# Latent values kept on chip, three units' values as fill, values stored in reading order

## The chip, the cores and the metric

The kernel is one program on one core of a Trainium2 chip. The metric is device time in microseconds (us); each kernel is run several times and the median is given. A matrix engine (TensorE, PE), a vector engine (VectorE, DVE), a scalar engine (ScalarE, ACT), a general engine (GpSimd, POOL) and a queue for transfers (SyncE, SP) each run their own instructions in order and wait for each other by semaphores; GpSimd issues transfers too. Tiles lie in on-chip memory, matmul results in 8 PSUM banks, everything else in DRAM.

## The reference, cut to what matters

Two networks run one after the other on 512 tokens of width 1024. The change touches the first, which has two layers. Each layer computes three kinds of attention from one projection, gates them and adds them:

```python
for l in range(DEPTH):                       # 2
    h = rms_norm(x, g_mix[l])
    proj = h @ w_in[l]
    c_q, c_kv, k_r, qkv_b, qkv_c, gate_logits = jnp.split(proj, IN_SPLITS, axis=-1)
    y_a = mla_mixer(c_q, c_kv, k_r, g_q[l], g_kv[l], w_uq[l], w_ukv[l])      # latent, 8 heads
    ...
    y_b = dilated_mixer(q_b, k_b, qkv_b[:, :, 2])                            # 3 groups of 4 heads
    ...
    y_c = neighbourhood_mixer(qkv_c[:, :, 0], qkv_c[:, :, 1], qkv_c[:, :, 2], rpb[l])   # 8 heads
    gates = jax.nn.sigmoid(gate_logits...).reshape(B, S, N_BRANCH, D_MODEL)
    merged = (gates[:, :, 0] * (y_a @ w_pa[l]) + gates[:, :, 1] * (y_b @ w_pb[l])
              + gates[:, :, 2] * (y_c @ w_pc[l]))
    x = x + merged @ w_o[l]
    h = rms_norm(x, g_ffn[l])
    x = x + (jax.nn.silu(h @ w1[l]) * (h @ w3[l])) @ w2[l]
```

In the latent mixer keys and values are products of a normed vector of 128 numbers per token, `kv = (rms_norm(c_kv, g_kv) @ w_ukv)`. The dilated mixer attends within a band over every 1st, 4th or 16th token. The neighbourhood mixer lays the tokens out as a grid of 8 rows and 64 columns; each query sees 8 rows by 16 columns of keys and adds a bias by relative place (`rpb`).

## The kernel before, in words

All products are made in three passes of a split in high and low parts (`mm3`, L264 to L268): high by high, high by low, low by high. `weights` (L255 to L262) loads 512 KB of weights on SyncE into one of two tiles `wst`, ScalarE copies the high part `whi`, the vector engine subtracts the low part `wlo` (three of each). `split` (L245 to L253) does the same for any tile: one ScalarE copy, one vector subtraction, here with a factor per row of tokens where one is needed.

Heads come in pairs. A "unit" is two pairs: units 0 to 2 are the dilated groups, 3 and 4 the neighbourhood heads. `unit` computes queries and keys of a pair (`put` splits and reorders them into eight `qk` tiles of 512 columns; copies of keys to the other half of the rows are GpSimd transfers, L551) and loads the pair's values into a tile V (two of them) by `v_load`. The values of all five units are made by `v_tokens`: units 0 and 1 in products of 512 columns in four banks (mm, mm, mm, T), units 2 and 3 likewise in banks T, S, S, O, unit 4 in products of 256 columns. Each block of 128 tokens by 256 columns is split into a tile `vn` and stored to DRAM (`vd`) on GpSimd's queue:

```python
vn = self.t(self.tp, "vn", (P, 4, 2, 64), F32R, bufs=2)
self.split(vn[:, :, 0], vn[:, :, 1], ps.rearrange("p (h d) -> p h d", h=4), scale)
self.nc.gpsimd.dma_start(out=dst, in_=vn.rearrange("p h x d -> p (h x d)").bitcast(F32))
```

The latent values go the same way through `vn` to `vda` (L751) and come back by `v_load` (L761) on SyncE. For the neighbourhood pairs `v_load` is eight transfers, one for each half of 32 grid columns by 4 grid rows.

`branches` sets the order. `latent` is the projection and roots of the latent mixer and its values; it is woven with `values` (all of `v_tokens`): `weave(main, fill, ratio)` takes from fill as much cost as the main yields times the ratio, and PAUSE (31000, 10000) in the main lets that much fill pass at two places, while the roots are computed. Then `stream` runs seven stretches of attention groups (latent pairs 0 to 2, latent pair 3, dilated 0 to 2, neighbourhood 0 and 1). A group is a score, a turn (the transposes of E, split into `ph` and `pl`) and a value product, and these follow each other with the lags LAG. The fill of a stretch is the next unit's queries and keys, then GATES[i] gates (products of 1024 by 128 weights, stored to `td` by SyncE), in the proportion `fills[i] / mains[i]`. The tile scheduler keeps this order on each engine.

The largest negated score of a row, `nmx`, and the row sum, `den`, are two small tiles; `stat_rows` (L499 to L513) transposes each of them on PE, copies it into `row`, and stores it, so that `inverse` can read the sums back spread over 64 rows (L524). The bias tables of a neighbourhood pair are three transfers per head (L1011).

## Time and profile before

| | |
|---|---|
| runs | 2510.02 us median of 3 (2508.36 to 2512.51) |
| profiled execution | 2510.62 us, of which the span of instructions is 2508.9 |
| mean granted clock of TensorE | 0.966 |
| instructions | 31833 |

The profile is of one execution. The windows divide it by time: latent starts of the two layers lie at 75 to 125 and 1050 to 1100 us, the neighbourhood stages at 375 to 525 and 1340 to 1490. In a window one sees how long each engine was busy in it and which share of its full clock the chip granted TensorE; 0.50 is 1.2 GHz, 1.0 is 2.4 GHz. The waits name the engine and line that waited and what ended the wait. A timeline row is one instruction with its start, its duration, and in brackets the idle time before it.

### The profile page before, as it was taken

Reading aid. Unit: us, or ns where it says so; the run is one execution under the profiler, and the core shown is the slowest. Engines: PE = TensorE matmul, PEld = TensorE weight load, DVE = VectorE, ACT = ScalarE, POOL = GpSimd, SP = SyncE. Lnnn points to the kernel's source line nnn. Section 1 sums busy time; section 2 is a strip of 40 time slices with the busy share of each in tenths; the row PEclk is TensorE's granted clock in tenths of the full one; section 3 lists DMA queues with packets and bytes.
Section 4 is the critical chain, followed back from the end, with each engine's and each line's share of the span. In section 5 each row is a group of like instructions: output and inputs, shape, how many; then the busy total and the mean of one; then the engine's idle time right before and its main releaser. Section 6 shows DMA issues by size and latency. Waiting matters only on the chain. (4 is left out here: it accounts for less than half of the span.)

```text
span 2508.9 us, 31833 instructions
## 1 busy us (share of the span) xinstructions
PE 2347.2 (94%) x11200; PEld 1937.8 (77%) x11200; DVE 1561.6 (62%) x2387; ACT 1171.0 (47%) x2072; POOL 724.0 (29%) x837
## 2 busy tenths in 40 slices
PE   8699998799999999889998889999999899979996
PEld 7588887588888888678887668878888788858874
DVE  6477787466444333567877657677433676697666
ACT  5366775344323223355776544323222466435653
POOL 3224355423111100224444623211112122142214
PEclk9799999799999999989999889999999999989998
DMA  5455556465333344454545556786334332224222
GB/s 188 162 167 137 158 148 174 155 214 190 104 96 98 94 138 130 139 186 136 175 138 159 172 178 203 231 267 224 125 113 147 107 108 83 86 90 123 73 80 76
DMA packets 147822, 362.00 MB, mean 144 GB/s; under 512 B 21104, under 2 KB 48528, under 8 KB 147664
## 3 DMA queue, kind: packets, MB, share of 16 engines
q1 hardware_dynamic: 124368, 300.36, 38.2%
q0 software_dynamic: 23296, 59.62, 7.8%
q8 instruction: 88, 1.44, 0.2%
q14 instruction: 70, 0.57, 0.1%
HBM read 286.78 MB, written 45.86 MB: 133 GB/s over the span
## 5 line engine op out<-in xcount | busy, mean ns | idle before, releaser
L248 ACT ACTIVATE whi<-wst 128x1024 fp32r<-128x1024 f32 (+4 forms) x387 | 374.0, 967 | 675.0 <-PE mm L267 179.5
L249 DVE TENSOR_TENSOR wlo<-wst,whi 128x1024 fp32r<-128x1024 f32 (+4 forms) x387 | 462.7, 1196 | 310.5 <-ACT whi L248 302.4
L266 PE MATMUL mm<-hh,whi 128*128 128x512 f32 x1184 | 473.3, 400 | 20.7 <-ACT whi L248 19.6
L268 PE MATMUL mm<-hh,wlo 128*128 128x512 f32 x1184 | 469.9, 397 | 0.3 <-DVE wlo L249 0.2
L267 PE MATMUL mm<-hl,whi 128*128 128x512 f32 x1184 | 468.4, 396 | 0.0
L266 PEld LDWEIGHTS mm<-hh,whi 128*128 128x128 f32 x1184 | 225.4, 190 | 64.8 <-ACT whi L248 20.5
L268 PEld LDWEIGHTS mm<-hh,wlo 128*128 128x128 f32 x1184 | 225.2, 190 | 48.3 <-DVE wlo L249 2.3
L267 PEld LDWEIGHTS mm<-hl,whi 128*128 128x128 f32 x1184 | 225.5, 190 | 43.7 <-issue 0.2
L699 POOL TENSOR_TENSOR s<-s,rf 128x512 f32<-128x512 f32 x44 | 75.5, 1718 | 401.0 <-ACT s L698 401.0
L363 PE MATMUL T<-ident,E 128*128 128x128 f32 x768 | 119.0, 277 | 16.8 <-DVE row L512 5.7
L363 PEld LDWEIGHTS T<-ident,E 128*128 128x128 f32 x768 | 93.4, 142 | 39.2 <-issue 8.9
L339 PE MATMUL S<-qk,qk 128*128 128x512 f32 (+2 forms) x512 | 110.8, 335 | 12.6 <-DVE nmx L346 12.0
L248 ACT ACTIVATE ph<-T 128x512 fp32r<-128x512 f32 x160 | 94.1, 596 | 57.1 <-PE T L363 55.7
L534 POOL DMA_DIRECT2D ry<-tmp x136 | 67.9, 505 | 137.6 <-ACT tmp L531 69.8
L249 DVE TENSOR_TENSOR pl<-T,ph 128x512 fp32r<-128x512 f32 x128 | 86.9, 681 | 24.1 <-ACT ph L248 23.7
L339 PEld LDWEIGHTS S<-qk,qk 128*128 128x128 f32 x512 | 81.1, 196 | 22.4 <-DVE nmx L346 13.2
L415 POOL TENSOR_TENSOR O<-O,ll 64x256 f32<-64x256 f32 x72 | 75.8, 1053 | 69.7 <-DVE O L414 68.1
L300 POOL TENSOR_TENSOR tmp<-tmp,tmp 128x512 f32<-128x512 f32 x26 | 42.1, 1619 | 171.8 <-ACT tmp L296 168.1
L348 ACT ACTIVATE E<-E,nmx 128x256 f32<-128x256 f32 (+1 forms) x160 | 72.8, 456 | 38.8 <-DVE nmx L346 38.4
L266 PE MATMUL S<-hh,whi 128*128 128x512 f32 x208 | 82.9, 398 | 5.8 <-ACT hh L251 5.8
L268 PE MATMUL S<-hh,wlo 128*128 128x512 f32 x208 | 82.6, 397 | 2.7 <-DVE wlo L249 2.7
L267 PE MATMUL S<-hl,whi 128*128 128x512 f32 x208 | 82.7, 398 | 0.0
(629 smaller groups left out, 5472.4 us busy)
## 6 DMA issues: line engine op xcount, KB each, us to landing
wst<-win SPq DMA_DIRECT2D x153, 512.0 KB
wst<-w SPq DMA_DIRECT2D x120, 512.0 KB
mw<-wada SPq DMA_DIRECT2D x48, 512.0 KB
td<-gate SPq DMA_DIRECT2D x48, 256.0 KB
vd<-vn POOLq DMA_DIRECT2D x40, 256.0 KB, 2.3
qk<-qk POOLq DMA_DIRECT2D x80, 128.0 KB, 3.5
V<-vd SPq DMA_DIRECT2D x80, 128.0 KB
ry<-tmp POOLq DMA_DIRECT2D x136, 64.0 KB, 3.7
```

The costliest lines, as they stand in the source:

```text
L248: nc.scalar.activation(hi, src, AF.Copy)
L249: nc.vector.tensor_tensor(lo, src, hi.bitcast(F32), op=ALU.subtract)
L266: mm(out, ah, bh, start=start, stop=False, **kw)
L267: mm(out, ah, bl, start=False, stop=False, **kw)
L268: mm(out, al, bh, start=False, stop=stop, **kw)
L300: self.nc.gpsimd.tensor_tensor(new, acc, sq, op=ALU.add)
L339: nc.tensor.matmul(sp[:, i * nk:(i + 1) * nk], a, b, start=n == 0, stop=n == len(ops) - 1)
L348: nc.scalar.activation(e[:, sl], e[:, sl], AF.Exp, scale=-1.0, bias=m, accum_out=d)
L363: nc.tensor.transpose(tp[:, i * P:(i + 1) * P], e[:, i * P:(i + 1) * P], self.ident)
L415: nc.gpsimd.tensor_tensor(dst, dst, lo, op=ALU.add)
L534: nc.gpsimd.dma_start(out=y[r:r + 32], in_=f[r ^ 32:(r ^ 32) + 32])
L699: nc.gpsimd.tensor_tensor(s, s, r, op=ALU.mult)
```

## The change

- The latent values are split straight into the two V tiles on chip, scaled by r3's column, from banks S, S, T, O. The tile holds pairs 0 and 1, or 2 and 3. There is no `vda`.
- Units 0 and 1 are still made first, 512 columns wide, and are stored as one block of 128x1024 per 128 tokens, through the `ph` and `pl` tiles. Units 2, 3 and 4 are made 256 columns wide; what the latent main does not use up is the first fill of stretch 0, whose `fills` grows by 26000. PAUSE and GATES change.
- Unit 2's values are stored in the order in which dilation 16 reads them, units 3 and 4's by grid column; keys of the neighbourhood units are ordered by grid column too, and so are the bias tables and masks, so that the 32 columns that a block of queries sees are one run of 256. The V loads become one or two per pair, on GpSimd's queue.
- A bias table is one transfer of 128x768 per head, prepared by the host in that order.
- `qk` tiles hold high and low parts together, so that a key copy is one transfer where two were. `nmx` and `den` are one tile `stats`; a dilated pair transposes and stores both at once. `spread` is a helper for transfers that were written out before.
- The square sums of r2 and r3 use bank O instead of mm.

```diff
-GATES = (3, 0, 6, 1, 1, 4, 1)
+GATES = (1, 0, 6, 1, 1, 4, 3)
-PAUSE = (31000, 10000)
+PAUSE = (12000, 9000)
...
     def stat_rows(self, stat, order, dst):
-        ps = self.bank("ms")
+        ps, n = self.bank("ms"), stat.shape[1]
...
+    def spread(self, out, d, offset):
+        for j in range(2):
+            self.nc.gpsimd.dma_start(out=out[64 * j:64 * j + 64], in_=bass.AP(d.tensor, d.offset + offset + j * S, [[0, 64], [1, S]]))
...
     def v_tokens(self, win, rc, vd):
...
-        for base, units, tags in ((24, (0, 1), ("mm", "mm", "mm", "T")), (28, (2, 3), "TSSO")):
...
+            self.v_store(ps[tk], rc()[:, tk:tk + 1], vd[sl[tk], 0:1024], "p" + "hl"[tk % 2])
+        for u in (2, 3, 4):
+            wt = [self.weights(win[24 + 2 * u + c]) for c in range(2)]
+            for tk in range(4):
...
+                    self.mm3(ps, self.hh[:, k, sl[tk]], self.hl[:, k, sl[tk]], wt[k // 4][0][:, o], wt[k // 4][1][:, o],
+                             k == 0, k == 7)
+                    yield 330
+                dst = at(8 * tk * w + 512 * u, (w, 8), (32 * w, 16), (1, 512)) if u == 2 else \
+                    at(2 * tk * w + 512 * u, (w, 2), (8 * w, 64), (1, 512))
+                self.v_store(ps, rc()[:, tk:tk + 1], dst, "vn")
...
-                self.nc.sync.dma_start(out=(v[:, s:s + i + cnt] if cnt > 1 else v[:, s + i]).bitcast(F32), in_=src)
+                self.nc.gpsimd.dma_start(out=(v[:, s:s + i + cnt] if cnt > 1 else v[:, s + i]).bitcast(F32), in_=src)
...
-            vd = st["vd"] = self.t(self.dr, "vda", (S, 1024), bufs=1)
+            vs = st["v"] = [self.t(self.tp, "V", (P, 8, 256), F32R, bufs=2) for _ in range(2)]
             for tk in range(4):
-                ps = self.bank("mm")
+                ps = self.bank("SSTO"[tk])
...
-                for hf in range(2):
-                    self.v_store(ps[:, hf * 256:hf * 256 + 256], rc3[:, tk:tk + 1], vd[sl, hf * 512:hf * 512 + 512])
-                yield 1500
+                for i, v in enumerate(vs):
+                    hi, lo = (v[:, 2 * tk:2 * tk + 2].rearrange("p n (j x d) -> p (n j) x d", j=2, x=2)[:, :, x] for x in range(2))
+                    self.split(hi, lo, ps[:, i * 256:i * 256 + 256].rearrange("p (h d) -> p h d", h=4), rc3[:, tk:tk + 1])
+                yield 650
...
-        cparts = [(2 * w_, [(64, 4), (1, 32)], (256, 2), KC0[w_]) for w_ in range(4)]
+        colrow = lambda ap: ap.rearrange("p (r c) -> p c r", r=8)
...
+                        nc.gpsimd.dma_start(out=bt, in_=a["rpb"][l, hd])
...
+        fills[0] += 26000
```

The vector engine's order at the start of the first layer's latent stage, before: the column sums of r3 are done (L313 stands just ahead), and the latent blocks (from mm banks, with `rc_113`) and the values of units 2 and 3 (from T, S and O, with `rc_251`) all go through `vn`.

```order
L252 SCALAR_TENSOR_TENSOR vn_686<-mm_682,rc_113_606,vn_686 128x4x64
L252 SCALAR_TENSOR_TENSOR vn_690<-mm_682,rc_113_606,vn_690 128x4x64
L252 SCALAR_TENSOR_TENSOR vn_694<-T_512,rc_251,vn_694 128x4x64
L252 SCALAR_TENSOR_TENSOR vn_698<-T_512,rc_251,vn_698 128x4x64
L252 SCALAR_TENSOR_TENSOR vn_702<-S_513,rc_251,vn_702 128x4x64
L252 SCALAR_TENSOR_TENSOR vn_706<-S_513,rc_251,vn_706 128x4x64
L252 SCALAR_TENSOR_TENSOR vn_710<-S_514,rc_251,vn_710 128x4x64
L252 SCALAR_TENSOR_TENSOR vn_714<-S_514,rc_251,vn_714 128x4x64
L252 SCALAR_TENSOR_TENSOR vn_718<-O_515,rc_251,vn_718 128x4x64
L252 SCALAR_TENSOR_TENSOR vn_722<-O_515,rc_251,vn_722 128x4x64
L252 SCALAR_TENSOR_TENSOR vn_752<-mm_748,rc_113_606,vn_752 128x4x64
L252 SCALAR_TENSOR_TENSOR vn_756<-mm_748,rc_113_606,vn_756 128x4x64
```

The same place after: units 0 and 1 in `ph` and `pl`, the two reciprocals, the first blocks of unit 2 in `vn`, and then the column sums of r3, which the V tiles wait for (two rows further the first `V_551<-S_559,rc_92_465`).

```order
L255 SCALAR_TENSOR_TENSOR ph_519<-mm_356,rc_251,ph_519 128x8x64
L255 SCALAR_TENSOR_TENSOR pl_523<-mm_357,rc_251,pl_523 128x8x64
L309 RECIPROCAL tmp_442<-tmp_443 128x512
L255 SCALAR_TENSOR_TENSOR ph_527<-mm_358,rc_251,ph_527 128x8x64
L255 SCALAR_TENSOR_TENSOR pl_531<-T_359,rc_251,pl_531 128x8x64
L252 TENSOR_TENSOR wlo_555<-wst_553,whi_554 128x512
L255 SCALAR_TENSOR_TENSOR vn_612<-mm_547,rc_251,vn_612 128x4x64
L252 TENSOR_TENSOR tmp_455<-tmp_452,tmp_454 128x512
L309 RECIPROCAL O_461<-tmp_462 128x512
L255 SCALAR_TENSOR_TENSOR vn_680<-mm_547,rc_251,vn_680 128x4x64
L252 TENSOR_TENSOR wlo_621<-wst_619,whi_620 128x640
L316 ISA tmp_466,rc_92_465<-O_461,ident 128x128
```

The ten `vn` blocks in a row are gone; the reciprocals have moved in between the blocks of values.

SyncE's order in the first layer's neighbourhood stage, before (`gate` and `td` are the gates' store, `wst` weights):

```order
L260 DMA wst_4444<-wpa 128x512
L584 DMA td_174<-gate_4171 128x512
L260 DMA wst_4474<-wpb 128x256
L761 DMA V_3792<-vd_182 128x1x256 x8
L584 DMA td_174<-gate_4234 128x512
L260 DMA wst_4492<-win 128x1024
L260 DMA wst_4536<-wpa 128x512
L584 DMA td_174<-gate_4332 128x512
```

And after, with the same gates and weights:

```order
L263 DMA wst_4348<-wpa 128x512
L591 DMA td_174<-gate_4146 128x512
L263 DMA wst_4380<-wpb 128x256
L602 DMA tmp_4144<-yd_173 128x512
L602 DMA tmp_4901<-yd_173 128x512
L263 DMA wst_4398<-win 128x1024
L591 DMA td_174<-gate_4200 128x512
L591 DMA td_174<-gate_4245 128x512
L263 DMA wst_4448<-wpa 128x512
```

The eight V loads ahead of the gate's store and the weights are gone from this queue.

GpSimd's order in that stage, before (`O` with `ll` is the sum that ends a value product, `RD` the inverse sums read back, `qk` key copies):

```order
L1013 TENSOR_TENSOR bias_4306<-bias_4306,maskc_3609 128x768
L713 DMA yd_173<-o_2087 128x512
L507 DMA rdd_4365<-row_4368 8x128
L415 TENSOR_TENSOR O_4034<-O_4034,ll_4220 64x32x8
L978 TENSOR_TENSOR O_2458<-O_2458,O_2967 128x512
L524 DMA RD_4067<-rdd_4061 64x512 x2
L1011 DMA bias_4752<-rpb 128x1x256 x3
L415 TENSOR_TENSOR O_4034<-O_4034,ll_4283 64x32x8
L524 DMA RD_4371<-rdd_4365 64x512 x2
L978 TENSOR_TENSOR O_2458<-O_2458,O_3408 128x512
```

And after, where the V tile of a neighbourhood pair is loaded:

```order
L1015 DMA bias_4122<-rpb 128x768
L521 DMA RD_3697<-fd_3651 64x512 x2
L558 DMA qk_3640<-qk_3640 64x1024
L769 DMA V_3635<-vd_182 128x4x256
L769 DMA V_3635<-vd_182 128x3x256
L417 TENSOR_TENSOR O_3479<-O_3479,ll_3968 64x32x8
L720 DMA yd_173<-o_2035 128x512
L986 TENSOR_TENSOR O_2395<-O_2395,O_2881 128x512
L521 DMA RD_3888<-rdd_3882 64x512 x2
L1016 TENSOR_TENSOR bias_4122<-bias_4122,maskc_3470 128x768
L417 TENSOR_TENSOR O_3855<-O_3855,ll_4041 64x32x8
```

The two V loads stand between the key copy and the next sum, and what is behind them on this engine is issued after them.

## Rows read from the trace of the kernel before

**Rows 1.** The page, busy time of each engine:

```profile
PE 2347.2 (94%) x11200; PEld 1937.8 (77%) x11200; DVE 1561.6 (62%) x2387; ACT 1171.0 (47%) x2072; POOL 724.0 (29%) x837
```

**Rows 2.** Windows: stretch, length, busy us of each engine, clock, DMA share, GB/s:

```profile
75.00:125.00 50.00, 26.15 (x138) 22.18 (x137) 21.50 (x40) 15.77 (x29) 12.36 (x23) 0.73 0.46 166
375.00:525.00 150.00, 124.35 (x574) 100.18 (x573) 91.49 (x177) 70.36 (x152) 71.56 (x87) 0.89 0.56 173
1050.00:1100.00 50.00, 27.89 (x148) 23.46 (x147) 23.05 (x44) 16.48 (x32) 14.40 (x27) 0.73 0.50 176
1340.00:1490.00 150.00, 124.17 (x586) 100.40 (x585) 92.98 (x180) 72.58 (x156) 72.40 (x89) 0.90 0.56 173
```

**Rows 3.** Windows, parts at granted clock 0.50: latent starts, then neighbourhood stalls:

```profile
sum 54.20, PE 16.18 PEld 13.19 DVE 15.95 ACT 14.27 POOL 17.31; mean PE 5.39 PEld 4.40 DVE 5.32 ACT 4.76 POOL 5.77
...
479.00:492.50 13.50, 6.14 (x14) 4.36 (x15) 3.38 (x4) 2.32 (x3) 2.46 (x4) 0.50 0.58 180
1448.40:1461.90 13.50, 5.86 (x13) 4.17 (x14) 2.86 (x4) 2.31 (x3) 2.44 (x4) 0.50 0.58 183
sum 54.00, PE 30.79 PEld 23.64 DVE 27.95 ACT 21.73 POOL 21.29; mean PE 7.70 PEld 5.91 DVE 6.99 ACT 5.43 POOL 5.32
```

**Rows 4.** PE's waits from 75 to 125: total, times, longest:

```profile
PE mm L266 <- DVE vn L252: 22.7, 4, 17.3
```

**Rows 5.** Timeline of ScalarE: start, duration, instruction, idle before:

```profile
88.82 0.47 ACT L251 ACTIVATE vn<-S,rc 128x256 fp32r<-128x256 f32 x1 [2.14 <-DMA vd<-vn]
```

**Rows 6.** PE's waits in the neighbourhood stretches, first layer, then second:

```profile
PE mm L266 <- ACT whi L248: 9.9, 1, 9.9
PE S L339 <- DVE nmx L346: 6.1, 2, 5.0
...
PE mm L266 <- ACT whi L248: 9.7, 1, 9.7
PE S L339 <- DVE nmx L346: 5.8, 2, 4.7
```

**Rows 7.** Timeline of SyncE's queue in the first layer's neighbourhood stage:

```profile
432.78 8.71 SPq L761 DMA_DIRECT2D V<-vd  x8
...
443.87 0.43 SPq L260 DMA_DIRECT2D wst<-win  x1
...
468.69 7.10 SPq L761 DMA_DIRECT2D V<-vd  x8
475.90 1.85 SPq L260 DMA_DIRECT2D wst<-win  x1
```

**Rows 8.** Timeline of ScalarE, the copies of those weights:

```profile
453.09 1.06 ACT L248 ACTIVATE whi<-wst 128x1024 fp32r<-128x1024 f32 x1 [11.74 <-DMA wst<-win]
...
485.21 1.06 ACT L248 ACTIVATE whi<-wst 128x1024 fp32r<-128x1024 f32 x1 [10.07 <-DMA wst<-win]
```

**Rows 9.** Timeline of the vector engine before the latent start:

```profile
65.95 0.69 DVE L249 TENSOR_TENSOR wlo<-wst,whi 128x512 fp32r<-128x512 f32 x1 [2.37 <-ACT whi L248]
66.56 3.35 DVE L306 RECIPROCAL tmp<-tmp 128x512 f32<-128x512 f32 x1
```

**Rows 10.** Timeline of PE, products of 256 and of 512 columns:

```profile
77.65 0.28 PE L266 MATMUL mm<-whi,hh 128*128 128x256 f32 x1
...
79.08 0.40 PE L266 MATMUL mm<-whi,bias 128*128 128x512 f32 x1
...
79.78 0.28 PE L266 MATMUL mm<-whi,hh 128*128 128x256 f32 x1
```

**Rows 11.** Lines of GpSimd: busy us, mean ns, idle before and its releasers:

```profile
L1011 POOL DMA_DIRECT2D bias<-rpb x48 | 25.7, 555 | 49.1 <-DVE nmx L346 24.7 <-PE mm L268 16.2 <-issue 8.1
```

**Rows 12.** The page, a DMA queue: packets, MB, share of 16 engines:

```profile
q0 software_dynamic: 23296, 59.62, 7.8%
```

**Rows 13.** Waits of SyncE's queue over the whole span: total, times, longest:

```profile
SPq L761 <- PE O L404: 31.9, 6, 10.9
SPq L761 <- PE T L404: 20.2, 6, 3.7
```

More of the change, by code (lines that the diff above doesn't have):

```diff
@@ L189, in _consts @@
     qc = (np.arange(P) // 8)[:, None]
[L190 removed]
+    kc = (np.arange(256) // 8)[None, :]
     mc = []
@@ L281, in dense, with ones_sum @@
             pass
-    def ones_sum(self, acc, ones=None):
+    def ones_sum(self, acc, ones=None, tag="mm"):
         sh = self.t(self.tp, "tmp", (P, S), F32R)
@@ L373, in turn @@
             if post and j == 1 and g == 4 // per - 1:
-                c["late"] = post(c["nmx"], c["den"])
+                c["late"] = post(c["st"])
             return 430
@@ L522, in inverse @@
         r = self.t(self.tp, "RD", (P, S), bufs=2)
-        for j in range(2):
-            nc.gpsimd.dma_start(out=r[64 * j:64 * j + 64], in_=bass.AP(d.tensor, d.offset + j * S, [[0, 64], [1, S]]))
+        self.spread(r, d, 0)
         return r
@@ L539, in rope, with put_pair @@
         return z
-    def put_pair(self, t, side, z, scale, order):
+    def put_pair(self, t, side, z, scale, order, both=None):
         for j in range(2):
@@ L549, in put_pair @@
             if side == 1:
-                for y in (x, t[4 + j]):
+                for y in (x, t[4 + j]) if both is None else (both[j],):
                     self.nc.gpsimd.dma_start(out=y[ot].bitcast(F32), in_=y[me].bitcast(F32))
@@ L718, in v_tokens @@
         sl = [slice(tk * P, (tk + 1) * P) for tk in range(4)]
-        def store(ps, tk, units):
-            for i, u in enumerate(units):
-                self.v_store(ps[:, i * 256:i * 256 + 256], rc()[:, tk:tk + 1], vd[sl[tk], u * 512:u * 512 + 512])
-        for base, units, tags in ((24, (0, 1), ("mm", "mm", "mm", "T")), (28, (2, 3), "TSSO")):
-            ps = [self.bank(x) for x in tags]
-            for k in range(8):
-                if k % 2 == 0:
-                    w = self.weights(win[base + k // 2])
-                o = slice(k % 2 * 512, k % 2 * 512 + 512)
-                for tk in range(4):
-                    self.mm3(ps[tk], self.hh[:, k, sl[tk]], self.hl[:, k, sl[tk]], w[0][:, o], w[1][:, o], k == 0, k == 7)
-                    yield 650
+        w = 2560
@@ L733, in v_tokens @@
+        at = lambda o, *ap: bass.AP(vd.tensor, vd.offset + o, [list(x) for x in ap])
+        ps = [self.bank(x) for x in ("mm", "mm", "mm", "T")]
+        for k in range(8):
+            if k % 2 == 0:
+                wt = self.weights(win[24 + k // 2])
+            o = slice(k % 2 * 512, k % 2 * 512 + 512)
             for tk in range(4):
-                store(ps[tk], tk, units)
-        w = [self.weights(win[32 + c]) for c in range(2)]
+                self.mm3(ps[tk], self.hh[:, k, sl[tk]], self.hl[:, k, sl[tk]], wt[0][:, o], wt[1][:, o], k == 0, k == 7)
+                yield 650
@@ new lines, in v_tokens @@
+        for u in (2, 3, 4):
+            wt = [self.weights(win[24 + 2 * u + c]) for c in range(2)]
+            for tk in range(4):
+                if tk % 2 == 0:
+                    bk = self.bank("mm")
+                ps = bk[:, tk % 2 * 256:tk % 2 * 256 + 256]
+                for k in range(8):
+                    o = slice(k % 4 * 256, k % 4 * 256 + 256)
+                    self.mm3(ps, self.hh[:, k, sl[tk]], self.hl[:, k, sl[tk]], wt[k // 4][0][:, o], wt[k // 4][1][:, o],
[4 more added lines that the diff above has]
+                self.v_store(ps, rc()[:, tk:tk + 1], dst, "vn")
@@ L839, in latent_pair @@
             w = self.weights(a["wuq"][l, p])
-            qh, ql, kh, kl = t = [qk_tiles(2) for _ in range(4)]
+            q, k = [[qk_tiles() for _ in range(2)] for _ in range(2)]
+            qh, ql, kh, kl = t = [[x[:, i] for x in y] for y in (q, k) for i in range(2)]
             ps = self.bank("mm")
@@ L859, in latent_pair, with f @@
                 self.split(qh[j], ql[j], qf)
-            st["pair", p] = t, self.v_load(st["vd"], p, 1024, [(0, [(1, P)], (P, 4), 0)])
+            st["pair", p] = t
         def finish(i, order, tap, stay=False):
-            def f(nmx, den):
-                rd = self.inverse(den)
+            def f(stats):
+                rd = self.inverse(stats[:, 1])
                 def late(o):
@@ L890, in unit @@
             for p in range(2):
-                t = qk_tiles(6)
+                q, *ks = [qk_tiles() for _ in range(3)]
+                t = [q[:, 0], q[:, 1]] + [x[:, i] for i in range(2) for x in ks]
                 for side in range(2):
@@ L972, in dil_merge @@
                     f = self.t(self.tp, "RD", (P, S), bufs=2)
-                    for j in range(2):
-                        nc.gpsimd.dma_start(out=f[rows(j)],
-                                          in_=bass.AP(fd.tensor, fd.offset + (g * 4 + 2 * p + j) * S, [[0, 64], [1, S]]))
+                    self.spread(f, fd, (g * 4 + 2 * p) * S)
                     nc.vector.tensor_tensor(outs[g, p], outs[g, p], f, op=ALU.mult)
@@ L1029, in early_outputs @@
         def early_outputs():
-            hi, lo = qk_tiles(2), qk_tiles(2)
+            hi, lo = ([x[:, i] for i in range(2)] for x in (qk_tiles(), qk_tiles()))
             for i in range(2):
@@ L1419, in attended, with f @@
         def attended(j):
-            def f(nmx, den):
-                nc.gpsimd.tensor_tensor(sg[j], sg[j], self.inverse(den), op=ALU.mult)
+            def f(stats):
+                nc.gpsimd.tensor_tensor(sg[j], sg[j], self.inverse(stats[:, 1]), op=ALU.mult)
                 def late(o):
```

104 lines of the change are left out of this document (45 added, 59 removed).

## The prediction

> **What bounds the kernel now.** I read the engine totals of the page first: the matmul engine is busy in 2347.2 of 2508.9 us and issues 11200 products [rows 1]. So nearly all that can be won without removing products is idle time of PE and time at its lower clock. The windows give both by stage; I took the 2 stretches of each layer that the diff touches. In them the reader is to see three numbers of a row: the length, PE's busy time, and the granted clock. The start of the latent stage has 50 − 26.15 = 23.85 us of idle PE in the first layer and 50 − 27.89 = 22.11 in the second; the two neighbourhood stretches have 150 − 124.35 = 25.65 and 150 − 124.17 = 25.83 [rows 2]. In parts of these stretches the granted clock is 0.50, the 1.2 GHz level of the two, each time in or behind a long pause of PE [rows 3]. PE's busy time in the parts at 0.50 is 16.18 us at the two latent starts and 30.79 us at the four neighbourhood stalls [rows 3], so half of it, 8.1 and 15.4 us, is what the clock costs.
>
> Then the waits. At the latent start PE waits 22.7 us for the vector engine's `vn`, 17.3 of it at once [rows 4]. `vn` itself is late since ScalarE cannot write it: the buffer (one of two) is still being stored to DRAM, with 2.14 us of waiting per pair of blocks [rows 5]. In the neighbourhood stretches the waits are 9.9 us for `whi` and 5.0 for `nmx` in the first layer, 9.7 and 4.7 in the second [rows 6]. For `whi` the cause stands on SyncE's queue: eight V loads take 8.71 us to issue at 432.78 and 7.10 at 468.69; the weight load behind the first is issued at 443.87, the one behind the second at 475.90 [rows 7]; ScalarE's copy of these weights starts at 453.09 and 485.21, after 11.74 and 10.07 us of waiting for the transfer [rows 8]. So 9.2 and 9.3 us pass between issue and use, with sixteen small V transfers on their way.
>
> **The latent start (term A).** The latent values no longer go through `vn`, DRAM and back: their splits write the two V tiles, 16 stores on GpSimd's queue and 8 loads on SyncE's go. Units 0 and 1 are stored as four 128x1024 blocks through four buffers where before eight halves went through two. Units 2 to 4 leave this stage and become fill for the latent attention. What A could give is the idle time and the clock: 23.85 + 22.11 + 8.1 = 54.1 us. Not all goes. The vector engine's order now has the two roots' reciprocals between the splits of `ph` and `pl`, `vn` and the column sums of r3; each takes 3.35 us [rows 9], and the values' eviction and the first queries stand behind them. Before, these lay beside the value products; now the stage has fewer products, so I let both come due: 2 × 3.35 = 6.7 us. And the first `wlo` of the latent weights is 2.37 us late, as the one there waits for `whi` now [rows 9]. So 9.07 us stay per layer, 18.1 in all, and A gives 54.1 − 18.1 = 36 us.
>
> **The neighbourhood stage (term B).** Its V loads were eight per pair, since each picked 32 grid columns; with values and keys in another order they are two, and stand on GpSimd's queue. SyncE then issues the gate's store and the weights when they are due. What goes is 9.9 + 5.0 + 9.7 + 4.7 = 29.3 us of waits [rows 6] and the 15.4 us of clock behind them, 44.7. At each of the four places the split of the weights still has to be made when they land; I leave one copy of 1.06 us [rows 8] at each, 4.2. So B gives 40.5 us.
>
> **The rest.** Units 2 and 3 were 96 products of 512 columns per layer and kind, now 192 of 256. In the trace twelve of 256 columns are 79.08 − 77.65 = 1.43 us, 0.119 each, and three of 512 are 0.70, 0.233 each [rows 10]: 192 × 0.119 = 22.8 against 22.4, three kinds 1.4 us per layer dearer at most. They are now beside attention, whose softmax leaves PE holes, which hides some of it. 36 fewer transposes of the statistics give back at most what so many products of 256 columns take, 36 × 0.119 = 4.3. I take the sum of the two as nothing, with ±4 kept for the range. Bias tables come in one transfer where three were, key copies in one where two were, so GpSimd loses 62 transfers a layer and gains 16 V loads. One such issue is 0.555 us on GpSimd [rows 11], one V load on SyncE was 8.71 / 8 = 1.09 [rows 7]; the gain is 62 × 0.555 − 16 × 1.09 = 17 us at least for an engine that is idle two thirds of the time [rows 1]; I take nothing for it. Two gates move from the first stretch to the last, where all that are left are computed anyway, and the value fill (26000 in the plan's units, five gates) takes their room; the work that hides each is attention's softmax, so nothing. Without that cover a gate is 24 products, 24 × 0.233 = 5.6 us.
>
> The stores in reading order are a price that no row shows: unit 2's is cut in 8 x 16 and the others' in 2 x 64. The trace's plain store keeps `vn` busy so that the next writer waits 2.14 us [rows 5]. If the odd ones take several times that, `vn` comes round only after two blocks, 48 products of 0.119, 5.7 us, and attention between them; I take nothing, and at the other end 3.5 us for each of 6 blocks and both layers, 42 us. The Trainium skill has a rule on this ("DMA: Bandwidth & Descriptors", section "Why a DMA increments its semaphore by 16 and not by 1"): the transfer is spread over the largest number of engines up to 16 that divides the slowest dimension of both sides, which would give the 2 x 64 stores two engines; it also tells of transfers issued by GpSimd that got 16 in spite of it. An estimate by that page: GpSimd's queue moved 59.62 MB in 7.8% of 16 engines' span [rows 12], so 19 GB/s on one, and 256 KB on two would be 6.9 us, still near the two blocks above; the sum would be the same.
>
> **The sum.** The profiled execution took 2510.62 us, 0.6 above the median of the runs. 2510.6 − 36 − 40.5 = 2434 us.
>
> **Rivals.** (1) All of it goes: idle time of the four stretches and all clock, 54.1 + 25.65 + 25.83 + 15.4 = 121, so 2390. For it: the fill has grown by 26000 units, so small waits have work to hide in. Against: some waits of the stretches are of other kinds [rows 2, 6] and nothing in the change touches them.
>
> (2) The vector engine is the limit where I blame transfers. It was 21.50 of 50 us busy at the start and 91.49 of 150 in the neighbourhood stretch [rows 2], and the second stall in each layer is put down to `nmx`, which it makes. Then half of the 17.35 at the latent start is still waited for, 8.7 per layer, and the `nmx` stalls with their clock stay: 5.0 + 4.7 + (30.79 − 6.14 − 5.86)/2 [rows 3]. That is 17.4 + 19.1 = 36.5, so 2470. Against: ScalarE's row before that wait names the weight transfer [rows 8].
>
> (3) The transfers share their engines whoever issues them. Then of the `whi` stalls only the issue goes, 7.10 of 9.9 and 9.7 [rows 6, 7]; 2.8 and 2.6 stay, and the pause is still followed by the lower clock, (6.14 + 5.86)/2 = 6.0 [rows 3]. B is 40.5 − 5.4 − 6.0 + 2.1 (the two copies counted above) = 31, so 2443. For it: 9.2 us from issue to use is far above the 0.4 us of issue. The Trainium skill says so ("DMA: Bandwidth & Descriptors", section "Issuing engines are not separate DMA queues"): another issuing engine saves only the time to issue. Here the number of transfers falls too, from eight to two a pair, which the rule doesn't speak of.
>
> (4) Slower. GpSimd runs in order, and a V load that waits for its tile now stops what is queued behind it: the sum of attention's output, the copies of keys, the bias tables, the spread of the inverse sums. On SyncE these waits were 31.9 + 20.2 us in 12 [rows 13], 4.34 each. 20 V tiles × 4.34 = 87 us passed whole to PE gives 2510.6 − 76.5 + 87 = 2521. It decides from 76.5 / 20 = 3.8 us a tile. Against: in the new order each V tile has some 20 us of products between its last reader and the next tile's first, and a wait on GpSimd has to outlast that before PE sees it.
>
> **How the numbers follow.** Forecast 0.46, rival 1 0.10, rival 2 0.18, rival 3 0.17, rival 4 0.09. The predicted time is 2434. The forecast's own range is 2424 to 2446 (±4 of small terms, a stall's 6 us more or less). The range that holds 8 in 10 runs from just above rival 1 to above rival 2 with part of the store's price: 2395 to 2482. About 0.2%, 5 us, is what a measurement of this kernel can tell from no change. Faster by more: all but rival 4 and cases near where it decides, 0.90; within 0.2%: 0.02; slower: 0.08.
>
> **What the profile after would show.** PE issues 11200 + 192 − 36 = 11356 products. At the latent starts no wait of PE for `vn` above 2 us, no rows of `vda`, and PE idle for 9 us in the place of 23; no long part at 0.50. In the neighbourhood stretches SyncE has no V rows, ScalarE's wait for the weights is gone, and the 9.9 us wait is not there. If it is there at 2.8, rival 3 holds; if `nmx` is still waited for 5 us, rival 2. GpSimd shows 32 V loads; PE waits whose releaser is GpSimd's sum or a key copy, behind one of them, would be rival 4. The forecast is wrong if PE's idle time at the latent start is above 15 us in a layer, or if a new wait of over 3 us stands in the middle of the attention stretches.

## The result and the profile after

The changed kernel takes 2434.18 us (median of 4 runs, 2432.9 to 2436.26) against 2509.19 us (4 runs, 2508.23 to 2512.51) for the kernel before on the same chip: 0.970 of it, 95% interval 0.9683 to 0.9716. The profiled execution took 2432.9 us, its span is 2431.1.

The page of the changed kernel, busy time of each engine, answers to [rows 1]:

```profile
PE 2325.6 (96%) x11356; PEld 1932.1 (79%) x11356; DVE 1571.2 (65%) x2367; ACT 1169.5 (48%) x2064; POOL 695.4 (29%) x745
```

PE issues 11356 products, 156 more, as counted. It is busy for 21.6 us less, mostly since less of its time runs at the lower clock, and its idle time fell from 161.7 to 105.5 us. These two are the whole gain of 77.8 us of span.

The windows of the changed kernel, columns as in [rows 2]: the two latent stages (start, then attention) of the first layer and of the second, then the neighbourhood stages with the products that follow each:

```profile
30.00:85.00 55.00, 50.75 (x262) 41.51 (x261) 45.45 (x70) 27.74 (x48) 13.20 (x16) 1.00 0.49 154
85.00:204.00 119.00, 110.39 (x683) 98.05 (x682) 81.89 (x126) 70.00 (x139) 34.56 (x49) 0.97 0.47 136
988.00:1040.00 52.00, 51.78 (x345) 46.75 (x344) 44.99 (x78) 35.40 (x69) 10.47 (x17) 1.00 0.55 154
1040.00:1140.00 100.00, 86.28 (x499) 73.67 (x498) 59.11 (x90) 50.50 (x100) 30.33 (x45) 0.97 0.47 140
...
330.00:490.00 160.00, 156.63 (x771) 130.50 (x770) 122.80 (x221) 94.18 (x197) 74.82 (x86) 0.98 0.62 199
490.00:533.70 43.70, 36.20 (x165) 28.54 (x164) 24.85 (x39) 15.66 (x30) 14.09 (x13) 1.00 0.58 184
1270.00:1420.00 150.00, 145.78 (x714) 120.96 (x713) 113.07 (x211) 86.16 (x182) 73.70 (x84) 0.98 0.61 197
1420.00:1468.00 48.00, 43.08 (x200) 34.29 (x199) 29.69 (x45) 19.13 (x36) 15.43 (x14) 1.00 0.57 181
```

The latent start is nearly full: 4.25 and 0.22 us of idle where 23.85 and 22.11 were. But idle time has moved into the latent attention behind it, 8.6 and 13.7 us. In the neighbourhood stages 3.4 and 4.2 us are left of 25.65 and 25.83; a new pause of 7.5 and 4.9 us stands where the attention ends. The parts at the lower clock (0.50 and a little more) are four of 6.8 us; their sums, first the two in the latent attention, then the two in the neighbourhood stages, are:

```profile
sum 13.60, PE 8.02 PEld 6.98 DVE 10.32 ACT 6.08 POOL 6.29; mean PE 4.01 PEld 3.49 DVE 5.16 ACT 3.04 POOL 3.15
...
sum 13.60, PE 11.67 PEld 9.83 DVE 13.37 ACT 7.59 POOL 7.12; mean PE 5.84 PEld 4.92 DVE 6.69 ACT 3.79 POOL 3.56
```

So A, by the prediction's own reckoning, is 54.1 − (4.25 + 8.61 + 0.22 + 13.72 + 8.02/2) = 54.1 − 30.8 = 23.3 us. In B the stalls and their clock in the neighbourhood stages go down to 3.4 + 4.2 + 11.67/2 = 13.4, and the pauses at the end take back 12.4. Before, the idle time there was 51.5 and all six parts at 0.50 had 40.17 us of PE busy, half of which is 20.1:

```profile
sum 63.90, PE 40.17 PEld 31.37 DVE 36.40 ACT 28.76 POOL 28.01; mean PE 6.70 PEld 5.23 DVE 6.07 ACT 4.79 POOL 4.67
```

so B is 71.6 − 13.4 − 12.4 = 45.8 us. The other 77.8 − 23.3 − 45.8 = 8.7 us lie in small pieces elsewhere; I did not trace them to one place. Part of them need not be the change's: PE's idle time from the end of the second layer's attention on (from 1541 us before, from 1468 us after) is 3.4 us less, where the change touches nothing.

What are the new pauses in the latent attention? The longest in the first layer, as rows of the changed kernel's timeline (PE, ScalarE, then four of GpSimd):

```profile
157.21 1.65 PE L341 MATMUL S<-qk,qk 128*128 128x512 f32 x3 [6.58 <-ACT E L353]
...
154.32 0.47 ACT L254 ACTIVATE vn<-mm,rc 128x256 fp32r<-128x256 f32 x1 [9.72 <-DMA vd<-vn]
...
138.00 4.63 POOL L1016 TENSOR_TENSOR bias<-bias,maskc 128x768 f32<-128x768 f32 x2 [9.78 <-DMA maskc<-maskC]
142.59 1.63 POOL L759 DMA_DIRECT2D vd<-vn  x2
144.21 0.55 POOL L510 DMA_DIRECT2D rdd<-row  x1
155.23 1.11 POOL L521 DMA_DIRECT2D RD<-rdd  x2 [10.47 <-DMA rdd<-row]
```

Read backwards: PE waits for ScalarE's exponential; ScalarE stood 9.72 us at a copy into `vn`, behind which the exponential was queued; `vn` was still being stored. Two of these stores were issued together at 142.59, after GpSimd had waited 9.78 us for the mask, and more than 11 us passed until `vn` was free. Even a row of statistics issued behind them is waited for 10.47 us. In the second layer, at the same stage, PE waits 8.24 us, but the chain is another: ScalarE stands only 3.76 us at `vn`, and it is the vector engine that holds PE up. It waits 10.87 us for the inverse sums that GpSimd reads back, and the row that they are read from was issued at 1075.05, behind two such stores:

```profile
1090.66 0.80 PE L271 MATMUL mm<-hh,wlo 128*128 128x512 f32 x1 [8.24 <-DVE wlo L252]
1088.78 0.69 DVE L877 TENSOR_TENSOR O<-O,RD 128x512 f32<-128x512 f32 x1 [10.87 <-DMA RD<-rdd]
1073.39 1.67 POOL L759 DMA_DIRECT2D vd<-vn  x2
1075.05 0.55 POOL L510 DMA_DIRECT2D rdd<-row  x1
1085.24 1.09 POOL L521 DMA_DIRECT2D RD<-rdd  x2 [9.64 <-DMA rdd<-row]
```

So two stores issued together, late, are the root in both layers. The page gives the median from issue to landing of each kind of transfer; here are the values' stores and loads of the changed kernel (GpSimd's queue; there is no V row of SyncE):

```profile
V<-vd POOLq DMA_DIRECT2D x20, 512.0 KB, 5.4
...
vd<-vn POOLq DMA_DIRECT2D x24, 256.0 KB, 9.4
...
V<-vd POOLq DMA_DIRECT2D x12, 384.0 KB, 5.7
...
vd<-ph POOLq DMA_DIRECT2D x4, 512.0 KB, 4.1
```

A store in reading order takes 9.4 us for 256 KB; twice as many bytes in plain order take 4.1. The 9.4 is a median over 24 stores of two shapes: the eight of unit 2 (8 x 16 rows) land in 4.3 to 6.1 us, the sixteen of units 3 and 4 (2 x 64 rows) in 8.5 to 12.5. In the kernel before, a plain store of the same size landed in 2.3:

```profile
vd<-vn POOLq DMA_DIRECT2D x40, 256.0 KB, 2.3
```

This is the price that no row of before showed.

### The profile page after: what moved, and what is told of

It is laid out like the page before. It is cut to its first block, busy times and chain, and to the rows that moved or that the text cites. A ratio compares the mean times of both kernels' runs of the same rounds, so it can differ in the third digit from the quotient of the medians.

```text
span 2431.1 us, 31714 instructions
## 1 busy us (share of the span) xinstructions
PE 2325.6 (96%) x11356; PEld 1932.1 (79%) x11356; DVE 1571.2 (65%) x2367; ACT 1169.5 (48%) x2064; POOL 695.4 (29%) x745
## 5 line engine op out<-in xcount | busy, mean ns | idle before, releaser
L252 DVE TENSOR_TENSOR wlo<-wst,whi 128x1024 fp32r<-128x1024 f32 (+4 forms) x387 | 471.4, 1219 | 257.4 <-ACT whi L251 256.7
L341 PE MATMUL S<-qk,qk 128*128 128x512 f32 (+2 forms) x512 | 108.1, 329 | 12.2 <-ACT E L353 12.2
L252 DVE TENSOR_TENSOR pl<-T,ph 128x512 fp32r<-128x512 f32 x128 | 87.2, 683 | 25.6 <-ACT ph L251 25.1
L350 ACT ACTIVATE E<-E,stats 128x256 f32<-128x256 f32 (+1 forms) x160 | 73.0, 457 | 51.9 <-DVE stats L348 51.4
```

Source lines behind the costliest of these rows:

```text
L252: nc.vector.tensor_tensor(lo, src, hi.bitcast(F32), op=ALU.subtract)
L341: nc.tensor.matmul(sp[:, i * nk:(i + 1) * nk], a, b, start=n == 0, stop=n == len(ops) - 1)
L350: nc.scalar.activation(e[:, sl], e[:, sl], AF.Exp, scale=-1.0, bias=m, accum_out=d)
```

## The experiments

All times are medians of 4 runs, each kernel on one chip with the kernel before, which took 2509.5 to 2514.2 us there. The changed kernel is 2434.2. I write what a run took off or added against that, or against the kernel before where it is built on that one. Small differences are to be read with care: the chips differ by up to 5 us, and stretches that no edit touches differ too. From the last value product of the second layer to the end, the same 4363 products take 981.0 us in the changed kernel's profiled execution, 988.3 in that of a_half and 987.7 in that of a_lat_dram.

**Stores in two halves (a_half).**

```diff
+        if len(dst.shape) == 3 and dst.shape[0] == 2:
+            for i in range(2):
+                self.nc.gpsimd.dma_start(out=dst[i], in_=src[64 * i:64 * i + 64])
+            return
```

> The changed kernel, but each store of units 3 and 4 in reading order is two transfers of 64 rows instead of one of 2 x 64. Theory (the odd store is slow): the median landing of vd<-vn, 9.4 us in the changed kernel, falls to about 4; ScalarE's waits for it in the latent attention (9.7 us in the first layer, 3.8 to 5.0 in the second) shrink below 2, and with them PE's pauses of 6.6 and 8.2 us and the lower clock behind them: 15 to 20 us faster than the changed kernel, 2414 to 2419 us. Rival (GpSimd's wait for the mask, 9.8 and 13.0 us, holds the stores back): PE's two pauses stay, 2430 to 2436 us.

2409.74 us: 24.4 off, more than expected. From the first score to the last latent value product the two layers take 127.2 and 129.7 us, where the changed kernel takes 139.5 and 147.0. The landing and the windows of the latent stage in this kernel (first its start, then the attention):

```profile
vd<-vn POOLq DMA_DIRECT2D x32, 128.0 KB, 3.5
```

```profile
30.00:85.00 55.00, 51.16 (x260) 42.33 (x259) 45.54 (x70) 27.54 (x46) 13.22 (x16) 0.97 0.50 154
85.00:204.00 119.00, 119.00 (x746) 105.88 (x745) 91.39 (x146) 77.85 (x157) 42.21 (x68) 1.00 0.50 147
```

The median half lands in 3.5 us (the four issued together behind the mask in the first layer take 6.2 to 6.9), and PE is busy in all of the 119 us. So the shape of the store made the new pause in the first layer: GpSimd still waits for the mask there (8.64 us), and without the slow store this is harmless. In the second layer that wait is gone too, since the order has moved, so the two are not told apart there. Nor did a run remove the mask's wait alone; in the changed kernel ScalarE also stood 4.96 us for a store without the mask (at 1044 us), and PE waited 1.2. The Trainium skill's rule that the prediction weighed ("DMA: Bandwidth & Descriptors", section "Why a DMA increments its semaphore by 16 and not by 1") would carry the store of 2 x 64 rows on two engines and each half on sixteen; the estimate that the prediction made from it, 6.9 us of transfer, fits with the 8.5 to 12.5 us to landing, and so does the order of the three shapes. How many engines a store used, no row shows; its exception for GpSimd's transfers does not show here.

**Wider stores in the kernel before (b_ph).** One part of the change alone, for units 0 to 3:

```diff
+            if len(units) == 2:
+                vn = self.t(self.tp, "p" + "hl"[tk % 2], (P, 8, 2, 64), F32R, bufs=2)
+                self.split(vn[:, :, 0], vn[:, :, 1], ps.rearrange("p (h d) -> p h d", h=8), rc()[:, tk:tk + 1])
```

> The kernel before with one edit: the values of units 0 to 3 are stored as 128x1024 blocks through the ph and pl tiles (four buffers of twice the size) instead of as 128x512 halves through vn (two buffers). Theory (the turnaround of two small buffers is what makes the latent start wait): the values of units 0 to 3 no longer wait, those of unit 4 and the latent ones still do; the wait of 17.3 us falls to 5 to 9, 18 to 28 us faster than before, 2482 to 2492 us. Rival (the vector engine is the limit there): 2505 to 2510 us.

2483.93 us, 25.6 off the kernel before. Its wait at the latent start, in the two layers together and as the longest single one:

```profile
PE mm L266 <- DVE vn L252: 15.4, 8, 3.7
```

Before, the longest was 17.3 [rows 4]. Two small buffers were the limit, not the vector engine: rival 2 of the prediction falls for this stage. (The edit makes the buffers both more and wider; which of the two counts is not told apart.)

**Latent values through DRAM again (a_lat_dram).** In the changed kernel, the latent blocks go through `vn` and come back:

```diff
-                for i, v in enumerate(vs):
...
+                for hf in range(2):
+                    self.v_store(ps[:, hf * 256:hf * 256 + 256], rc3[:, tk:tk + 1], vda[sl, hf * 512:hf * 512 + 512], "vn")
...
+            st["pair", p] = t, self.v_load(st["vda"], p, 1024, [(0, [(1, P)], (P, 4), 0)])
```

> The changed kernel, but the latent values go to DRAM through vn in 8 stores per layer and come back by one V load per latent pair on GpSimd's queue, as in the kernel before. Theory (the two vn buffers are the limit at the latent start): eight rotations of about 3.6 us for two come back ahead of the first value product, and the fill that could hide them needs vn too: 10 to 20 us per layer, 2452 to 2472 us. Rival (the larger fill hides it): 2434 to 2440 us.

2460.99 us: 26.8 added, inside the theory's range. The first value product comes 22.3 and 21.9 us after the first score of its layer, in the changed kernel 12.8 and 11.6. By the end of the latent attention the layers have lost 13.8 and 7.3 us; another 6.7 lie behind all attention, where the edit touches nothing. PE's own waits there name `vn` for only 1.6 us in the first layer, so the way from the buffers to PE is not shown line by line; nor are the eight V loads, which are back too, told apart from the buffers. So both halves of term A are shown apart, as edits: fewer and wider blocks, and no latent values in them.

**The plan's numbers (a_plan).** GATES and PAUSE of before in the changed kernel.

> The changed kernel with the plan's numbers of before: GATES (3, 0, 6, 1, 1, 4, 1) and PAUSE (31000, 10000). Theory (the numbers only shift fill between places that are covered): 2428 to 2440 us. Rival (with the long pause the values of units 2 to 4 are spent ahead of the latent attention, which then has too little fill): pauses of PE in the latent attention, 2445 to 2460 us.

2441.49 us: 7.3 added, between the two ranges. PE's waits in the first layer's latent stage are of the rival's kind, though shorter:

```profile
PE mm L269 <- DVE vn L255: 9.8, 4, 5.1
```

With the long pause more value blocks queue for the two `vn` ahead of the latent attention: up to its first score the first layer has 18.0 us of idle PE, the changed kernel 9.5. In exchange PE has no idle time from there to the last latent value product in either layer, where the changed kernel has 10.0 and 13.7: the new pauses hang on the plan as well, which puts these stores beside the latent attention. The sum of both is worth 7 us, no more than untouched stretches differ by.

**The V loads: queue, number, pattern.** Five kernels. First the loads of the kernel before moved to GpSimd, nothing else:

```diff
-                self.nc.sync.dma_start(out=(v[:, s:s + i + cnt] if cnt > 1 else v[:, s + i]).bitcast(F32), in_=src)
+                (self.nc.gpsimd if len(parts) == 4 else self.nc.sync).dma_start(out=(v[:, s:s + i + cnt] if cnt > 1 else v[:, s + i]).bitcast(F32), in_=src)
```

> The kernel before with one edit: the eight V loads of each neighbourhood pair are issued by GpSimd instead of SyncE. Theory (SyncE's queue is what held the weights): the waits of 9.9, 9.7, 5.0 and 4.7 us and the clock behind them go, 35 to 45 us faster than before, 2465 to 2475 us. Rival (the transfers share their engines whoever issues them): only the time to issue goes, 7 us of each of the two long waits, 2485 to 2497 us. If GpSimd held up by the V loads costs more than that: above 2500 us.

2495.63 us, 13.9 off the kernel before: the rival's range. PE's waits in its first neighbourhood stretch:

```profile
PE S L339 <- DVE nmx L346: 6.1, 2, 5.1
PE O L404 <- DVE O L414: 5.9, 4, 2.6
PE mm L266 <- ACT whi L248: 2.5, 2, 2.1
```

The wait for `whi` fell from 9.9 [rows 6] to 2.1 us (in the second layer from 9.7 to 1.9), so SyncE's queue did hold the weights. But new waits, 5.9 us in all, stand before the value products, and the stall before `nmx` stays at its old length, with another cause. In the kernel before the vector engine stood 7.64 us for a gate tile whose store was issued behind the V loads; here GpSimd issues the loads for 5.45 us and the inverse sums that it reads back come behind them, which is 2.29 of the 5.1 us (the rest is the vector engine's work in between):

```profile
451.79 0.69 DVE L578 TENSOR_TENSOR gate<-mm,r 128x512 f32<-128x512 f32 x1 [7.64 <-DMA td<-gate]
```

```profile
424.67 5.45 POOL L761 DMA_DIRECT2D V<-vd  x8
430.11 1.10 POOL L974 DMA_DIRECT2D RD<-fd  x2
```

```profile
437.94 0.69 DVE L976 TENSOR_TENSOR o<-o,RD 128x512 f32<-128x512 f32 x1 [2.29 <-DMA RD<-fd]
```

(The first fence is the kernel before, the other two this one.) This is the prediction's rival 4 in small: what waits behind a V load on GpSimd is late. The Trainium skill says that another issuing engine saves only the time to issue ("DMA: Bandwidth & Descriptors", section "Issuing engines are not separate DMA queues"); the wait for `whi` fell by 7.8 us in each layer, about the 7.10 us that the loads took to issue ahead of it [rows 7], and the kernel gained no more than two such times, so this pair of runs agrees.

Then the other way round, the changed kernel's two loads a pair back on SyncE (a_v_sp):

> The changed kernel with its V loads (one or two per pair) back on SyncE's queue. Theory (what counts is that a V load waiting for its tile, and its transfer, stand ahead of the weights): waits of PE for whi come back in the neighbourhood stretches, 3 to 6 us each with the clock behind them, 2445 to 2460 us. Rival (what counted was the number of transfers, eight against two): SyncE issues two in about 1 us, 2434 to 2439 us.

2445.93 us: 11.7 added, inside the theory's range, though by other waits than it named: no wait for `whi` is among the long ones; there are waits of 3.6 us for a row of statistics in each neighbourhood stage, and one of the latent attention's grew from 8.2 to 11.4. Seven loads of 128 rows instead of two, on GpSimd (a_v7):

```diff
+                if pair >= 6:
+                    for j in range(cnt):
+                        src = bass.AP(vd.tensor, vd.offset + (t0 + j * sp[0]) * width + pair * 256, [[width, P], [1, 256]])
+                        self.nc.gpsimd.dma_start(out=v[:, s + j].bitcast(F32), in_=src)
+                    continue
```

> The changed kernel, but the V tile of each neighbourhood pair is loaded in seven transfers of 128x1x256 on GpSimd's queue instead of two, the same bytes from the same places. Theory (the number of transfers is what most of the gain of the neighbourhood stage hangs on): five more issues of 0.7 us on GpSimd per pair, key copies and sums behind them late, PE's waits of 2 to 5 us come back: 2442 to 2456 us. Rival (only that the loads are off SyncE's queue, and the bytes, count): 2432 to 2438 us.

2424.0 us: 10.2 off where I expected time to be added. My theory that many loads cost time is wrong here. What the five more loads did, by the trace, is to move other work: the vector engine's first merge of the dilated outputs, which waits for its factors, stands later in the order. In the changed kernel it holds the vector engine for 4.61 us and PE for 3.37; with seven loads it comes 8 us later and waits for nothing. First the row of the changed kernel, then that of this one:

```profile
376.53 0.69 DVE L984 TENSOR_TENSOR o<-o,RD 128x512 f32<-128x512 f32 x1 [4.61 <-DMA RD<-fd]
```

```profile
384.85 0.68 DVE L989 TENSOR_TENSOR o<-o,RD 128x512 f32<-128x512 f32 x1
```

The last two ask about the pattern: seven loads on SyncE, of 128 rows in a run (a_7_sp) or of four runs of 32 rows with gaps (a_g7_sp):

```diff
-                        src = bass.AP(..., (t0 + j * sp[0]) * width + pair * 256, [[width, P], [1, 256]])
+                        src = bass.AP(..., (32 * (s + j)) * width + pair * 256, [[64 * width, 4], [width, 32], [1, 256]])
```

> The changed kernel with all V loads on SyncE's queue and each neighbourhood pair's tile loaded in seven transfers of 128 rows that follow each other. Theory now (what held the weights in the kernel before was not the number of the loads but that each read four runs of 32 rows with gaps): no more than 8 us off the run with two loads on SyncE (2445.9), 2438 to 2454 us. Rival (seven issues ahead of the weights are what cost): PE's waits for whi of 4 to 7 us come back in each layer with the clock, 2458 to 2475 us.

> As a_7_sp, but each of the seven transfers reads four runs of 32 rows with gaps of 32, the source pattern of the kernel before; the rows land in other places than the keys, so the neighbourhood output is not the reference's. Number, bytes, queue and program order are those of a_7_sp. Theory (a source of four runs is carried by few of the engines, and the weights that come behind wait there): waits for whi of 7 to 10 us come back, 20 to 45 us slower than a_7_sp, 2462 to 2495 us. Rival (the shape is nothing): within 4 us of a_7_sp.

2451.46 and 2463.66 us: the first as the theory had it; the second 12.2 slower, the theory's direction, but little more than half of the least it named. In the stretch that the edit touches (last latent value product to last value product) the two layers are 11.0 and 9.3 us longer. The way is not the one named either: no long wait for `whi` came back; in the first layer PE waits 4.5 us for a row of statistics and 4.1 for the sums of a value product. One V tile on SyncE's queue in the one and in the other:

```profile
437.29 3.17 SPq L771 DMA_DIRECT2D V<-vd  x7
440.50 0.43 SPq L642 DMA_DIRECT2D E<-td  x1
```

```profile
445.26 6.13 SPq L771 DMA_DIRECT2D V<-vd  x7
451.43 1.25 SPq L642 DMA_DIRECT2D E<-td  x1
```

Seven loads of whole runs are issued in 3.17 us, 0.45 each; seven of four runs in 6.13 (5.4 to 10.8 for the other tiles), and the transfer behind them takes longer to issue too. So the pattern of the source has a price of its own, beside the queue.

**More transfers on GpSimd (a_g7_sp_many).** On top of that, bias tables in three and key copies in two again:

```diff
-                for y in (x, t[4 + j]) if both is None else (both[j],):
+                for y in (x, t[4 + j]):
...
+                        for ty in range(3):
+                            nc.gpsimd.dma_start(out=bt[:, ty * 256:ty * 256 + 256], in_=a["rpb"][l, hd][:, ty * 256:ty * 256 + 256])
```

> As a_g7_sp (V loads of four runs on SyncE; the neighbourhood output is not the reference's), and GpSimd's transfers are again as many as before: each bias table in three, each key copy in two. Queue and source pattern together brought back 24 of the 59 us that the neighbourhood stretches gained; the run asks where the rest is. Theory (the many small transfers on GpSimd): most of the rest comes back, 2480 to 2500 us. Rival (the rest lies in what stands behind the V loads on SyncE, small weights now where 512 KB were needed at once before, so in the order): 2461 to 2471 us.

2465.53 us, 1.9 from a_g7_sp, the rival's range: with the V loads on SyncE, the smaller number of transfers on GpSimd, a part of the change in its own right, is worth nothing that can be measured. Of the 58 us that the stalls of the neighbourhood stages gave up (71.6 to 13.4), queue and pattern brought back some 24 by the windows (a_g7_sp as a whole is 29.5 us above the changed kernel). The rest, some 34 us, would lie in what stands behind the loads in the order (behind the tile shown above a_g7_sp loads 128 KB of weights, at 452.79 us; in [rows 7] it is 512 KB, needed at once). That is by elimination: no run put that order back, and it stays open.

**The end of the attention (a_half_drain, a_best).** In the changed kernel the last stretch's fill is used up when two groups still have their turns and values to do. The kernel before has no pause there: the 24 products of a gate still stand behind its last value product (547.2 to 552.6 us in the first layer); why its fill reaches further, no run shows. These kernels spread the fill over the two groups (LAG[1] steps more, the ratio times 0.85); both have the two halves of the stores.

```diff
-            self.weave(chain.from_iterable(advance((g, after if i == len(gs) - 1 else None)) for i, g in enumerate(gs)),
-                       fill, ratio)
+            more = [None] * b if n == last else []
+            self.weave(chain.from_iterable(advance((g, after if i == len(gs) - 1 else None) if g else None)
+                                           for i, g in enumerate(gs + more)), fill, ratio)
```

> The changed kernel with the 64-row stores, and the last stretch's fill is spread over the last two groups' turns and values too (the ratio times 0.85), which come after the fill in the changed kernel. Theory (PE's idle 7.5 and 4.9 us at the end of the attention is that those have nothing beside them): 5 to 11 us below the kernel with 64-row stores alone (2409.7), 2399 to 2405 us. Rival (the scheduler already places the next products there, and the wait is for the output's own split): 2406 to 2413 us.

2389.28 us, but this time isn't to be compared: the edit also took the last two groups' turns and values out of the second network's attention. Its first network is whole, and there the pause at the end is gone. The two windows where a_half has 2.7 and 4.5 us idle, of a_half first, then of this kernel:

```profile
475.00:515.00 40.00, 37.32 (x170) 29.86 (x169) 21.22 (x36) 15.79 (x31) 9.11 (x10) 0.96 0.55 178
1396.00:1436.00 40.00, 35.48 (x164) 28.26 (x164) 22.44 (x35) 15.99 (x31) 13.49 (x13) 1.00 0.55 178
```

```profile
475.00:518.00 43.00, 43.00 (x200) 35.62 (x199) 27.35 (x37) 16.98 (x28) 14.55 (x13) 1.00 0.63 204
1385.00:1428.00 43.00, 43.00 (x200) 35.61 (x199) 27.45 (x39) 17.54 (x31) 13.74 (x14) 1.00 0.62 191
```

Then all three edits, with the second network as it was (a_best):

> The changed kernel with three edits: stores of units 3 and 4 in two transfers of 64 rows, neighbourhood V tiles in seven loads on GpSimd, and the first network's last stretch spreads its fill over the last two groups too (ratio times 0.85). Theory (the three add up: 24 for the stores, 10 for the loads, 5 to 11 for the end): 2388 to 2398 us. Rival (the loads' gain was a shift of GpSimd's order that the stores' edit shifts again, and the end is bound by the output's own split): 2400 to 2410 us.

2382.61 us (2378.83 to 2384.7), 0.9485 of the kernel before (0.9468 to 0.9502) and 51.6 below the changed kernel: more than the parts added up. Its windows of the latent attention and the neighbourhood stage with what follows, first layer:

```profile
85.00:204.00 119.00, 118.94 (x743) 105.64 (x742) 89.78 (x145) 77.58 (x155) 41.99 (x68) 1.00 0.50 147
320.00:508.60 188.60, 188.60 (x938) 158.00 (x936) 143.56 (x258) 109.05 (x224) 97.22 (x118) 1.00 0.66 210
```

PE waits for nothing there, at the full clock. That is the time of the prediction's rival 1 (2390 us) and less, reached by three edits more.

## Why the prediction was right, and where it was not

The time was forecast as 2434 and is 2434.2. That is closer than the working deserves: its two terms missed in opposite ways, and 8.7 us came from elsewhere.

- **Term A, forecast 36, measured 23.3.** The cause was right: b_ph and a_lat_dram show that the two `vn` buffers made the latent start wait. What I left there was wrong in place. The 18.1 us that I put down to reciprocals and the first `wlo` are 4.5 in fact; the vector engine fits them beside the value products (45.45 of 55 us busy). The step that failed is the store in reading order, which I took at nothing, arguing that two blocks and attention between them would cover a late `vn`. With the stores' issue delayed by the mask, they don't: in the first layer ScalarE, in order, holds the exponential behind the copy into `vn`; in the second the row of statistics waits behind the stores and the vector engine waits for it. These stores land in 8.5 to 12.5 us, where the cover that I counted on was two blocks, 5.7 us, and the attention between them. The latent attention loses 22.3 us of idle and 4.0 of clock; in a_half the idle time is gone, and that kernel is 24.4 us faster. The other end of the price, 42 us, was in the text, and the range held it.
- **Term B, forecast 40.5, measured 45.8.** The four stalls and their clock go, and more than I counted: 58.2 of 71.6 us. Against it stands a pause of 12.4 us at the end of the attention, of which I had no step. Its cause was named only after the fact: that two groups run bare. a_half_drain and a_best show that more fill there removes it; why the kernel before had fill left at that place stays open.
- **Why B goes.** I gave the place of the loads on SyncE's queue as the cause. That holds for the waits for `whi`, but moving them alone is worth 13.9 us (b_v_pool). Their source pattern is worth 12.2. Their number did not bring those waits back: seven in place of two took off 10.2 us on GpSimd (a_v7) and added 5.5 on SyncE (a_7_sp against a_v_sp), which is within what untouched stretches differ by. The bias tables and key copies are worth nothing that can be measured. That leaves some 34 us for which the cause is not shown. The stall that the profile put down to `nmx` had its cause one step further back, in a gate tile not yet stored; following that chain in the trace of before would have told me.
- **Rival 1** (2390) didn't come with this change, but a_best is below it: 2382.6. **Rival 2** is refuted at the latent start, and in the neighbourhood stages the changed kernel has no wait of PE left for `nmx` (`stats` there). **Rival 3** describes b_v_pool, not the change, in which the pattern changes too. **Rival 4** (slower) didn't come: in the changed kernel GpSimd never stands more than 1.84 us before a V load; but its mechanism shows in b_v_pool and, with the mask in the place of a V tile, in the pause at 157.
- Of the signs that I named, the products, the missing `vda` and SyncE's missing V rows are as said. The one for a wrong forecast also came: waits of over 3 us in the middle of the attention (6.58 and 8.24 in the latent stages, 3.37 and 3.94 in the neighbourhood stages). The time hid it.

## What to carry to other kernels

When a change makes a transfer's pattern odd to save the reader work, price the writer's buffer by that transfer's own landing time: where one of 2 x 64 rows landed in 8.5 to 12.5 us, cutting it into pieces of 64 rows removed the pause. (More buffers are the other way; no run here tried them.) An engine in order passes such a delay to whatever is queued behind it, so follow the chain one step beyond the instruction that the wait names, and in each layer anew: the same stores held PE up by ScalarE in one and by the vector engine in the other. And a total that comes out right proves no term of it; compare stage by stage.

## What was not expected of the hardware

- Two stores of 64 rows landed in a median of 3.5 us each (6.9 at most behind the mask) where one of 2 x 64 rows took 8.5 to 12.5, on the same queue; one of 8 x 16 rows took 4.3 to 6.1, a plain one of the same size 2.3 in the kernel before.
- Seven loads whose sources are four runs of 32 rows are issued by SyncE in 5.4 to 10.8 us where seven of 128 rows in a run take 3.2 to 4.9.
- Seven V loads a pair instead of two made the kernel 10 us faster, in its trace by shifting the scheduler's order of other work: a run that changes a number of instructions also changes the order, and its time holds both.
